# Three plain and accumulating loads per seven-product block move to GpSimd's queue

## The chip, the core and the metric

The kernel runs on one core of a Trainium2 chip. The time is the device time of one execution in microseconds, as a median of several runs. The core has engines that run side by side: TensorE (PE) multiplies matrices, VectorE (DVE) and ScalarE (ACT) work element by element, GpSimd (POOL) and SyncE (SP) here do little but issue DMA transfers. Transfers that SP issues go through the DMA queue q1 (hardware_dynamic in the profile), those that POOL issues through q0 (software_dynamic). Both queues use the same 16 DMA engines.

## The reference

One layer of a hybrid decoder in float32, with 256 tokens of width 2048: a gated feed-forward network (FFN1) at half weight, a token mixer, a second feed-forward network (FFN2), and a last normalisation.

```python
def swiglu_ffn(x, w_gate, w_up, w_down):
    return (jax.nn.silu(x @ w_gate) * (x @ w_up)) @ w_down
...
    x = x + FFN_RESIDUAL_SCALE * swiglu_ffn(rms_norm(x, ffn1_norm[l]),
                                            ffn1_w_gate[l], ffn1_w_up[l], ffn1_w_down[l])
    z = rms_norm(x, mix_norm[l]) @ w_in[l]
...
    x = x + y @ w_out[l]
    x = x + FFN_RESIDUAL_SCALE * swiglu_ffn(rms_norm(x, ffn2_norm[l]),
                                            ffn2_w_gate[l], ffn2_w_up[l], ffn2_w_down[l])
return rms_norm(x, final_norm)
```

The feed-forward width is 5632, so each of the six large matrices holds 46 MB. Left out above is what turns z into y: a gated linear recurrence (RG-LRU) and a short convolution.

## The kernel before

**Numbers.** Each float32 factor is split in two parts, hi and lo, and a product is hi·hi + lo·hi + hi·lo. For a weight block of 1 MB (128 partitions x 4 x 512 numbers), `load` (lines 159 to 168) has SP fetch it into a buffer called raw; `parts_of` (lines 180 to 190) then has ACT cast it to hi in two pieces and DVE compute lo = raw − hi; PE multiplies. A raw buffer is free for the next load when DVE is through with lo. The streamed blocks share three such buffers.

**Stages.** Each feed-forward network has five steps s = 0 to 4, each with a gate block (names g1_s or g2_s, the first number is that of the network) and an up block (u1_s, u2_s); after s = 0, 2 and 4 a down product follows (d1_1, d1_5, d1_9, and d2_... alike). Between the networks the mixer runs, which the change does not touch.

**Seven products.** `seven` (line 396) computes a product of 2 x 2 blocks of weights with seven instead of eight block products. For that it needs sums of weight blocks: w12 + w11, then + w22, then − w11, then + w21. Two more buffers, tagged "kept", hold what lives through the block: `run` is the running sum, `w11` the first block. The start of `run` is made by the DMA itself: SP loads w12 (line 412, through `get`), and then POOL issues an accumulating load (line 413) that adds w11 to what stands in the buffer. Then SP loads w11 again by itself into the other kept buffer (line 414). The remaining blocks (`b2`, `w22`, `b3`, `a2`, `w21`, `a3`) are streamed by SP through the three raw buffers. In the names of buffers 01 is w12 and `run`, 00 is w11, 11 is w22, 10 is w21, and 21, 31, 20, 30 are b2, b3, a2, a3. Down blocks have other first digits (raw_d2_1_11 is the running sum of d2_1, raw_d2_1_10 its w11).

The products go in the order: `run` (p4), w11 (p0), b2, `run` + w22 (p5), b3, run − w11 (p6), w22 (p2), a2, run + w21 (p3), a3, w21 (p1). PE takes 12 or 24 matmuls for each.

**Order and waits.** The scheduler of the framework sets the order of instructions on each engine from the program's order and the dependencies; each engine and each issuing queue works strictly in its order. `run` takes the kept buffer that is free after p6 of the previous block, w11 the one free after its p3. The accumulate waits until the plain load of `run` has landed. The first gate block of FFN1 has its inputs in place already (`ready`); the other 25 calls of `seven` take the path that the change touches: 9 gate, 10 up and 6 down blocks.

After each gate and up block, the result is transposed by DMA: `part` (line 203) has SP issue a transposing transfer from the buffer `pair`, so these stand in SP's queue among the loads.

Of the kernel before, what the change touches and what calls it, by code (L numbers as in the profile page):

```python
# [10 lines left out]
F32 = mybir.dt.float32  # L11
# [3 lines left out]
ALU = mybir.AluOpType  # L15
AX = mybir.AxisListType

P = 128
# [6 lines left out]
CW = 512  # L25
NC_D = D // CW
UK = 4
# [22 lines left out]
def hybrid_block(ctx: ExitStack, tc: tile.TileContext, a: dict, out: bass.AP):  # L50
    nc = tc.nc
# [31 lines left out]
    def bank(name):  # L83
        return psum.tile([P, 512], F32, tag="ps", name=name)

    def f32(ap):
        return ap.bitcast(F32)
# [68 lines left out]
    extra = []  # L156
    turn_of = {"split": 0}

    def load(src, name, pieces=((0, UK),), loaded=None, kept=False):
        if kept:  # L160
            raw = extra[1].tile([P, UK, CW], F32, tag="kept", name=f"raw_{name}", bufs=2)
        else:
            raw = raws.tile([P, UK, CW], F32, tag="raw", name=f"raw_{name}")
        for i, e in pieces:
            nc.sync.dma_start(raw[:, i:e, :], src[i * P : e * P].rearrange("(j p) c -> p j c", p=P))
            if loaded:
                loaded(i)
        return raw

    def splits_of(name):  # L170
        pool, bufs = splits, 2
        if extra:
            turn_of["split"] += 1
            if turn_of["split"] % 3 == 0:
                pool, bufs = extra[0], 1
        hi = pool.tile([P, UK, CW], F32R, tag="hi", name=f"hi_{name}", bufs=bufs)
        lo = pool.tile([P, UK, CW], F32R, tag="lo", name=f"lo_{name}", bufs=bufs)
        return hi, lo, [(hi[:, j, :], lo[:, j, :]) for j in range(UK)]

    def parts_of(raw, name, pieces=((0, 2), (2, UK)), split=None):  # L180
        hi, lo, blk = splits_of(name)
        for i, e in pieces:
            if split:
                split(i)
            act.copy(hi[:, i:e, :], raw[:, i:e, :])
            if split:
                dve.tensor_tensor(lo[:, i:e, :], raw[:, i:e, :], f32(hi[:, i:e, :]), op=ALU.subtract)
        if not split:
            dve.tensor_tensor(lo, raw, f32(hi), op=ALU.subtract)
        return blk  # L190
# [4 lines left out]
    def stationary(tile, t):  # L195

        return [(tile[:, j, t * P : (t + 1) * P], tile[:, j, S + t * P : S + (t + 1) * P]) for j in range(UK)]
# [33 lines left out]
    def multiply(targets, blk, apart=False, middle=None):  # L231


        more = dict(skip_group_check=True) if apart else {}
        for ps, st, begin, _ in targets:
            for j in range(UK):
                pe.matmul(ps, st[j][0], blk[j][0], start=begin and j == 0, stop=False, **more)
                pe.matmul(ps, st[j][1], blk[j][0], start=False, stop=False, **more)
        if middle:
            middle()  # L240
        for ps, st, _, end in targets:
            for j in range(UK):
                pe.matmul(ps, st[j][0], blk[j][1], start=False, stop=end and j == UK - 1, **more)
        if len(targets) == NT:
            onward()
# [150 lines left out]
    def seven(w, rows, cols, sf, xs, name, keep, done, between=None, ready=None, whole=True, seeded=True):  # L396


        a, c, e, d = (bank(f"ps_{name}_{n}") for n in "aced")

        def of(u, n):
            return w[u * UK * P : (u + 1) * UK * P, cols[n] : cols[n] + CW]

        def get(u, n, kept=False):
            return load(of(u, n), f"{name}_{u}{n}", kept=kept)

        (r0, r1), two = rows, len(xs) > 1
        if ready:
            w11, first = ready
            run = get(r0, 1, True)  # L410
        else:
            run, first = get(r0, 1, True), None
            nc.gpsimd.dma_start(run, of(r0, 0).rearrange("(j p) c -> p j c", p=P), accum_op=ALU.add)
            w11 = get(r0, 0, True)
        b2, w22 = get(xs[0][0], 1), get(r1, 1)
        b3 = get(xs[1][0], 1) if two else None
        a2, w21 = get(xs[0][0], 0), get(r1, 0)
        a3 = get(xs[1][0], 0) if two else None

        def snap(ps, n, sign=1.0):  # L420
            s = keep(f"{n}_{name}")
            act.activation(s, ps, AF.Copy, scale=sign)
            return s

        def product_of(i, raw, ps, begin=False, end=True, blk=None):
            multiply([(ps, sf[i], begin, end)], blk or parts_of(raw, f"{name}_p{i}"), True)

        def usual(i, raw, n, *targets):

            blk = parts_of(raw, f"{name}_x{i}{n}")  # L430
            multiply([(ps, stationary(xs[i][1], t), b, z) for ps, t, b, z in targets], blk, True)

        def corner():
            product_of(0, w11, a, True, blk=first)
            if whole:
                act.copy(d, a)
                return []
            return [snap(a, "s1")]

        if ready:  # L440
            s1 = corner()
            hi, lo, blk = splits_of(f"{name}_p4")
            for i in (0, 2):
                o = slice(i, i + 2)
                dve.tensor_tensor(run[:, o], run[:, o], w11[:, o], op=ALU.add)
                act.copy(hi[:, o], run[:, o])
            for i in (0, 2):
                o = slice(i, i + 2)
                dve.tensor_tensor(lo[:, o], run[:, o], f32(hi[:, o]), op=ALU.subtract)
            product_of(4, run, c, True, blk=blk)  # L450
            s5 = [snap(c, "s5")]
        else:
            product_of(4, run, c, True)
            if seeded:
                act.copy(e, c)
            s5 = [] if seeded else [snap(c, "s5")]
            s1 = corner()
        if between:
            between(0)
        usual(0, b2, 1, (e, 1, not seeded, not two), (c, 0, False, False))  # L460
        if between:
            between(1)
        dve.tensor_tensor(run, run, w22, op=ALU.add)
        product_of(5, run, a)
        u2 = snap(a, "u2", -1.0)
        if between:
            between(2)
        if two:
            usual(1, b3, 1, (e, 1, False, True), (c, 0, False, False))
        dve.tensor_tensor(w11, run, w11, op=ALU.subtract)  # L470
        product_of(6, w11, a)
        u3 = snap(a, "u3", -1.0)
        done(1, 1, e, [u3] + s5)
        product_of(2, w22, c)
        done(0, 1, c, [u2])
        usual(0, a2, 0, (d, 0, not whole, False), (a, 1, False, False))
        dve.tensor_tensor(run, run, w21, op=ALU.add)
        product_of(3, run, a, end=not two)
        if two:
            usual(1, a3, 0, (a, 1, False, True), (d, 0, False, False))  # L480
        done(1, 0, a, [])
        product_of(1, w21, d)
        done(0, 0, d, s1)

    def ffn(tag, norm, after, opening=False):
        with (
# [252 lines left out]
            def down(last):  # L739
# [64 lines left out]
                if tag == 1 and m == 5:  # L804
                    prepare()
                seven(
                    wd, (m, n), (2 * CW, CW), sh, [(u, hidden[u]) for u in others], f"d{tag}_{m}", keep, add,
                    within,
# [419 lines left out]
```

## Time and profile before

| | |
|---|---|
| time, median of 3 runs | 1800.07 us (1798.57 to 1800.27) |
| the profiled execution's own time | 1805.48 us |
| its span, first to last instruction | 1803.7 us |
| mean granted TensorE clock | 0.984 |
| PE busy | 1725.1 us (96%) |
| DVE, ACT, POOL busy | 1380.5, 1204.4, 38.8 us |
| loads from SP | 261 of the feed-forward weights, 1 MB each, median 6.1 to 7.0 us from issue to landing |
| accumulating loads from POOL | 25, 1 MB each, median 11.6 to 12.9 us |

How to read the rows. A group of instructions has its line, engine and operation, then what it writes and reads, and how often it occurs. In a timeline a row begins with the start and the length in microseconds and ends, in brackets, with the idle time ahead of it and what ended this. In a list of waits the numbers are the total, the count, and the longest. "DMA to landing" is the time from the issue of a transfer to its end, smallest, median and largest. PEclk is the granted clock, where 1 is full speed. Nearly all rows name line 43, that of a helper that records every operation, so the names of the buffers tell the places.

### The profile page before, as it was taken

To read this page: it belongs to the slowest core of one execution; us is meant where nothing else is said; L and a number is where in the kernel's file an instruction comes from. 1 tells how busy PE (TensorE), PEld (TensorE's weight loads), DVE (VectorE), ACT (ScalarE), POOL (GpSimd) and SP (SyncE) were. 2 spreads that over 40 slices of the span, in tenths; PEclk is the share of its full clock that TensorE was granted. 3 is DMA by queue.
4 is the path that set the end of the run, shared out by engine and by line. 5 is a ranking of instruction groups with operands and counts; after the bars stand their busy time and mean duration, and the time that the engine had idled before them with its cause. 6 is when DMAs were issued, how large, how long until landed. Compare 5 with 4: busy or idle time off the path is not lost.

```text
span 1803.7 us, 19492 instructions
## 1 busy us (share of the span) xinstructions
PE 1725.1 (96%) x7471; PEld 1405.2 (78%) x7471; DVE 1380.5 (77%) x1118; ACT 1204.4 (67%) x1501; POOL 38.8 (2%) x45
## 2 busy tenths in 40 slices
PE   8999998999998989999999999899999999999998
PEld 6887787878876777888888887677778778878786
DVE  8977877768767758768696669769868687778686
ACT  7857566665556657877777776666657574667574
POOL 1000000000000000000000000000000000000000
PEclk9999999999999999999999999999999999999999
DMA  8776677795667684775666695696768668677863
GB/s 305 203 224 203 210 243 201 246 252 164 224 210 200 216 234 159 230 244 187 209 199 210 197 293 164 198 257 184 255 194 247 201 203 257 210 221 222 234 209 117
DMA packets 267373, 389.32 MB, mean 216 GB/s; under 512 B 86292, under 2 KB 88720, under 8 KB 267152
## 3 DMA queue, kind: packets, MB, share of 16 engines
q1 hardware_dynamic: 253616, 360.75, 62.1%
q0 software_dynamic: 13520, 26.29, 8.4%
q8 instruction: 58, 0.95, 0.2%
q10 hardware_dynamic: 144, 1.05, 0.1%
q14 instruction: 35, 0.29, 0.0%
HBM read 366.03 MB, written 2.10 MB: 204 GB/s over the span
## 4 chain that ended last, share of the span: by engine, by line
PE 64%; DMA 15%; DVE 9%; ACT 6%; issue 5%; SPq 0%; DVEq 0%; ACTq 0%
PE ps_in L43 11%; PE ps_d L43 10%; PE ps_g_a L43 6%; DMA raw_u<-in_ffn_w_up_dram 5%; PE ps_g_c L43 5%; PE ps_u_c L43 4%; DMA raw_g<-in_ffn_w_gate_dram 4%; DMA u_g<-pair 4%; PE ps_o L43 4%; PE ps_d_a L43 3%; PE ps_g_e L43 3%; PE ps_g_d L43 3%; PE ps_u_e L43 3%; PE ps_u_a L43 3%; PE ps_d_c L43 3%
## 5 line engine op out<-in xcount | busy, mean ns | idle before, releaser
L43 ACT CAST hi_u_p<-raw_u 128x1024 fp32r<-128x1024 f32 x140 | 143.8, 1044 | 92.6 <-DMA raw_u<-in_ffn_w_up_dram 36.5
L43 DVE TENSOR_TENSOR lo_u_p<-raw_u,hi_u_p 128x2048 fp32r<-128x2048 f32 x70 | 160.0, 2286 | 34.3 <-ACT hi_u_p L43 33.6
L43 ACT CAST hi_g_p<-raw_g 128x1024 fp32r<-128x1024 f32 x136 | 137.4, 1045 | 55.9 <-PE ps_g_a L43 16.4
L43 PE MATMUL ps_d<-hi_d,h 128*128 128x512 f32 x704 | 172.0, 397 | 1.9 <-ACT hi_d L43 1.9
L43 DVE TENSOR_TENSOR lo_g_p<-raw_g,hi_g_p 128x2048 fp32r<-128x2048 f32 (+1 forms) x69 | 155.1, 2254 | 17.6 <-ACT hi_g_p L43 17.2
L43 PEld LDWEIGHTS ps_d<-hi_d,h 128*128 128x128 f32 x704 | 135.6, 193 | 31.7 <-ACT hi_d L43 2.8
L43 PE MATMUL ps_in<-hi_in,xT_nm 128*128 128x512 f32 x640 | 152.3, 390 | 0.1
L43 ACT CAST hi_u_x<-raw_u 128x1024 fp32r<-128x1024 f32 x80 | 82.2, 1046 | 88.2 <-DMA raw_u<-in_ffn_w_up_dram 60.3
L43 PEld LDWEIGHTS ps_in<-hi_in,xT_nm 128*128 128x128 f32 x640 | 119.4, 188 | 25.1 <-ACT hi_in L43 0.6
L43 DVE TENSOR_TENSOR lo_u_x<-raw_u,hi_u_x 128x2048 fp32r<-128x2048 f32 x40 | 91.4, 2286 | 46.4 <-ACT hi_u_x L43 46.4
L43 DVE TENSOR_TENSOR lo_in<-raw_in,hi_in 128x2048 fp32r<-128x2048 f32 x40 | 91.2, 2286 | 43.0 <-ACT hi_in L43 42.6
L43 ACT CAST hi_g_x<-raw_g 128x1024 fp32r<-128x1024 f32 x80 | 80.6, 1044 | 49.3 <-PE ps_g_c L43 17.8
L43 DVE TENSOR_TENSOR lo_d<-raw_d,hi_d 128x2048 fp32r<-128x2048 f32 x44 | 100.5, 2287 | 16.4 <-ACT hi_d L43 16.4
L43 DVE TENSOR_TENSOR lo_g_x<-raw_g,hi_g_x 128x2048 fp32r<-128x2048 f32 x40 | 91.3, 2283 | 25.9 <-ACT hi_g_x L43 25.9
L43 ACT CAST hi_d_p<-raw_d 128x1024 fp32r<-128x1024 f32 x84 | 85.2, 1045 | 35.0 <-PE ps_d_a L43 9.7
L43 ACT CAST hi_d<-raw_d 128x1024 fp32r<-128x1024 f32 x88 | 88.6, 1044 | 17.6 <-DMA raw_d<-in_ffn_w_down_dram 9.3
L43 DVE TENSOR_TENSOR raw_u<-raw_u,raw_u 128x2048 f32<-128x2048 f32 x30 | 68.7, 2291 | 40.9 <-DMA raw_u<-in_ffn_w_up_dram 40.6
L43 DVE TENSOR_TENSOR lo_d_p<-raw_d,hi_d_p 128x2048 fp32r<-128x2048 f32 x42 | 95.8, 2285 | 4.9 <-ACT hi_d_p L43 4.8
L43 ACT CAST hi_in<-raw_in 128x1024 fp32r<-128x1024 f32 x80 | 80.8, 1046 | 26.9 <-PE ps_in L43 21.9
L43 PE MATMUL ps_d<-lo_d,h 128*128 128x512 f32 x352 | 87.2, 389 | 0.0
L43 DVE TENSOR_TENSOR h<-pair,h 128x512 fp32r<-128x512 f32 x44 | 30.3, 689 | 71.5 <-ACT h L43 71.3
L43 PE MATMUL ps_in<-lo_in,xT_nm 128*128 128x512 f32 x320 | 79.0, 389 | 0.0
(405 smaller groups left out, 3716.6 us busy)
## 6 DMA issues: line engine op xcount, KB each, us to landing
raw_d<-in_ffn_w_down_dram SPq DMA_DIRECT2D x88, 1024.0 KB, 6.1
raw_u<-in_ffn_w_up_dram SPq DMA_DIRECT2D x87, 1024.0 KB, 7.0
raw_g<-in_ffn_w_gate_dram SPq DMA_DIRECT2D x86, 1024.0 KB, 6.3
raw_in<-in_w_in_dram SPq DMA_DIRECT2D x40, 1024.0 KB, 5.1
raw_o<-in_w_out_dram SPq DMA_DIRECT2D x16, 1024.0 KB, 5.2
raw_u<-in_ffn_w_up_dram POOLq DMA_DIRECT2D x10, 1024.0 KB, 11.6
raw_g<-in_ffn_w_gate_dram POOLq DMA_DIRECT2D x9, 1024.0 KB, 12.9
raw_d<-in_ffn_w_down_dram POOLq DMA_DIRECT2D x6, 1024.0 KB, 12.6
```

The costliest lines, as they stand in the source:

```text
L43: ins = getattr(self.engine, name)(*args, **kwargs)
```

## The change

The three transfers for the kept buffers are issued by POOL, in this order: the plain load of w12 into the running sum, the accumulating load of w11 onto it, the plain load of w11. SP's queue holds all the others. The waits on buffers are the same as before, and so is the arithmetic.

```diff
         else:
-            run, first = get(r0, 1, True), None
-            nc.gpsimd.dma_start(run, of(r0, 0).rearrange("(j p) c -> p j c", p=P), accum_op=ALU.add)
-            w11 = get(r0, 0, True)
+            run, first = extra[1].tile([P, UK, CW], F32, tag="kept", name=f"raw_{name}_sum", bufs=2), None
+            for n, how in ((1, {}), (0, dict(accum_op=ALU.add))):
+                nc.gpsimd.dma_start(run, of(r0, n).rearrange("(j p) c -> p j c", p=P), **how)
+            w11 = extra[1].tile([P, UK, CW], F32, tag="kept", name=f"raw_{name}_first", bufs=2)
+            nc.gpsimd.dma_start(w11, of(r0, 0).rearrange("(j p) c -> p j c", p=P))
         b2, w22 = get(xs[0][0], 1), get(r1, 1)
```

SP's order where block u1_1 of FFN1 ends and g1_2 begins (u1_1's last loads, 20, 10 and 30, then g1_2's first; L208 is the transposing transfer), before:

```order
L165 DMA raw_u1_1_20_1855<-in_ffn1_w_up_dram 128x4x512
L165 DMA raw_u1_1_10_1857<-in_ffn1_w_up_dram 128x4x512
L165 DMA raw_g1_2_01_2123<-in_ffn1_w_gate_dram 128x4x512
L165 DMA raw_u1_1_30_1859<-in_ffn1_w_up_dram 128x4x512
L165 DMA raw_g1_2_21_2128<-in_ffn1_w_gate_dram 128x4x512
L208 DMA_TRANSPOSE u3_g1_1_1720<-pair_107 128x8x128
L165 DMA raw_g1_2_00_2126<-in_ffn1_w_gate_dram 128x4x512
L165 DMA raw_g1_2_11_2130<-in_ffn1_w_gate_dram 128x4x512
```

and in the changed kernel:

```order
L165 DMA raw_u1_1_20_1855<-in_ffn1_w_up_dram 128x4x512
L165 DMA raw_u1_1_10_1857<-in_ffn1_w_up_dram 128x4x512
L165 DMA raw_u1_1_30_1859<-in_ffn1_w_up_dram 128x4x512
L165 DMA raw_g1_2_21_2128<-in_ffn1_w_gate_dram 128x4x512
L208 DMA_TRANSPOSE u3_g1_1_1720<-pair_107 128x8x128
L165 DMA raw_g1_2_11_2130<-in_ffn1_w_gate_dram 128x4x512
```

The loads of g1_2's running sum (01) and of its w11 (00) are gone from SP's queue; the rest keeps its order.

POOL's order over the same place, with the block before and the one behind, before:

```order
L413 DMA raw_u1_1_01_1844<-in_ffn1_w_up_dram 128x4x512
L413 DMA raw_g1_2_01_2123<-in_ffn1_w_gate_dram 128x4x512
L413 DMA raw_u1_2_01_2410<-in_ffn1_w_up_dram 128x4x512
```

and now (x2 is the plain load with the accumulate behind it):

```order
L414 DMA raw_u1_1_sum_1844<-in_ffn1_w_up_dram 128x4x512 x2
L416 DMA raw_u1_1_first_1847<-in_ffn1_w_up_dram 128x4x512
L414 DMA raw_g1_2_sum_2123<-in_ffn1_w_gate_dram 128x4x512 x2
L416 DMA raw_g1_2_first_2126<-in_ffn1_w_gate_dram 128x4x512
L414 DMA raw_u1_2_sum_2410<-in_ffn1_w_up_dram 128x4x512 x2
L416 DMA raw_u1_2_first_2413<-in_ffn1_w_up_dram 128x4x512
```

POOL had one transfer per block and now has three; w11's load stands behind the accumulate.

SP's order behind block u2_0, where the down product of FFN2 begins (d2_1_0_2 and d2_1_3_0 are single blocks of it), before:

```order
L165 DMA raw_d2_1_0_0_8457<-in_ffn2_w_down_dram 128x4x512
L208 DMA_TRANSPOSE u3_g2_0_8050<-pair_107 128x8x128
L165 DMA raw_d2_1_10_8650<-in_ffn2_w_down_dram 128x4x512
L165 DMA raw_d2_1_0_2_8494<-in_ffn2_w_down_dram 128x4x512
L208 DMA_TRANSPOSE u2_g2_0_7989<-pair_107 128x8x128
L165 DMA raw_d2_1_3_0_8532<-in_ffn2_w_down_dram 128x4x512
```

and now:

```order
L165 DMA raw_d2_1_0_0_8457<-in_ffn2_w_down_dram 128x4x512
L208 DMA_TRANSPOSE u3_g2_0_8050<-pair_107 128x8x128
L208 DMA_TRANSPOSE u2_g2_0_7989<-pair_107 128x8x128
L165 DMA raw_d2_1_0_2_8494<-in_ffn2_w_down_dram 128x4x512
L165 DMA raw_d2_1_3_0_8532<-in_ffn2_w_down_dram 128x4x512
```

Here the second transpose moves ahead of a load as well, and w11 of d2_1 (raw_d2_1_10) no longer stands in front of it. PE's order is the same in both kernels.

## The prediction

> **What bounds the kernel now.** I read the engines' busy time first, then the chain of waits, then what TensorE waited for.
>
> ```profile
> span 1803.7 us, 19492 instructions
> PE 1725.1 (96%) x7471; PEld 1405.2 (78%) x7471; DVE 1380.5 (77%) x1118; ACT 1204.4 (67%) x1501; POOL 38.8 (2%) x45
> ...
> PE 64%; DMA 15%; DVE 9%; ACT 6%; issue 5%; SPq 0%; DVEq 0%; ACTq 0%
> ...
> PE ps_u_a L43 <- ACT hi_u_x L43: 11.7, 8, 2.8
> ```
>
> TensorE (PE) is the bound: 96% of the span, so at most 78.6 us of idle time can be won, plus what a lowered clock costs. The largest waits name ACT, but ACT itself was waiting. One stall, at 284 us, shows for what:
>
> ```profile
> L165 SPq DMA_DIRECT2D raw_u<-in_ffn_w_up_dram x1: 367/367/367, 274.8 to 274.8; - x1
>   ACT hi_u_x L43: 10.6, 1
> DMA to landing us min/median/max: 10.8/10.8/10.8
> ...
> 273.77 1.28 POOL L413 DMA_DIRECT2D raw_g<-in_ffn_w_gate_dram  x1 [38.52 <-DMA raw_g<-in_ffn_w_gate_dram]
> ...
> 286.83 1.20 PE L43 MATMUL ps_u_a<-hi_u_x,x 128*128 128x512 f32 x4 [2.45 <-ACT hi_u_x L43]
> ```
>
> Block u1_1's last streamed load (`a3`, named raw_u1_1_30) is issued by SP at 274.8, 1.0 us behind the accumulating load that POOL issued at 273.77 for the next block. It needs 10.8 us; ACT waits for it, and PE for ACT. Six places have this form, and one table prices them:
>
> ```profile
> 283.00:293.00 10.00, 6.85 (x23) 0.83 0.86 253
> 505.00:512.00 7.00, 5.33 (x22) 1.00 0.82 312
> 603.00:611.00 8.00, 6.99 (x31) 1.00 0.86 299
> 645.00:657.00 12.00, 8.95 (x32) 0.86 0.84 254
> 1343.00:1354.00 11.00, 8.67 (x25) 0.70 0.80 245
> 1431.00:1440.00 9.00, 5.86 (x19) 0.81 0.70 213
> sum 57.00, PE 42.64; mean PE 7.11
> ```
>
> The columns are the stretch, its length, PE's busy time, the granted clock, DMA share and GB/s. PE is idle 57.00 − 42.64 = 14.4 us there, and the clock below 1 costs 10×0.17 + 12×0.14 + 11×0.30 + 9×0.19 = 8.4 us: 22.8 us together.
>
> Why is the load slow? While both transfers run, the engines give the two queues the same number of packets, and the accumulate's packets are the dearer ones:
>
> ```profile
> q0 software_dynamic: 477, 0.95, 64.6%
> q1 hardware_dynamic: 548, 1.10, 40.9%
> ```
>
> (window 277 to 285 us). That is not so when the streamed load is nearer behind the accumulate. Two like places, near the end and in the middle:
>
> ```profile
> L165 SPq DMA_DIRECT2D raw_u<-in_ffn_w_up_dram x1: 367/367/367, 1685.4 to 1685.4; - x1
> DMA to landing us min/median/max: 6.0/6.0/6.0
> ...
> 1684.96 1.29 POOL L413 DMA_DIRECT2D raw_d<-in_ffn_w_down_dram  x1 [38.82 <-DMA raw_d<-in_ffn_w_down_dram]
> ...
> L165 SPq DMA_DIRECT2D raw_u<-in_ffn_w_up_dram x1: 367/367/367, 1333.6 to 1333.6; - x1
> DMA to landing us min/median/max: 11.4/11.4/11.4
> ...
> 1332.51 1.30 POOL L413 DMA_DIRECT2D raw_g<-in_ffn_w_gate_dram  x1 [39.34 <-DMA raw_g<-in_ffn_w_gate_dram]
> ```
>
> 0.4 us behind the accumulate the load lands after 6.0 us; 1.1 us behind it, after 11.4. The load that comes early enough goes first and the accumulate waits. Between 0.4 and 1.0 us lies a point of decision, and the change moves the accumulate by about that much.
>
> **The change, part by part.** 25 blocks are touched (10 up, 9 gate, 6 down); 50 plain loads leave SP for POOL.
>
> *1. The running sum's plain load starts later.* POOL starts later behind what it waits for than SP does. The plain load of g1_2 shows by how much:
>
> ```profile
> L165 SPq DMA_DIRECT2D raw_g<-in_ffn_w_gate_dram x1: 368/368/368, 267.1 to 267.1; - x1
> DMA to landing us min/median/max: 6.0/6.0/6.0
> ```
>
> It lands at 273.1 and POOL's instruction begins at 273.77: 0.65 us. The plain load inherits this, and so does the accumulate behind it. Where does it show?
>
> ```profile
> L413 POOL DMA_DIRECT2D raw_u<-in_ffn_w_up_dram x10: 1292/1293/1372, 79.8 to 1644.8; - x10
>   ACT hi_u_p L43: 32.1, 7
> DMA to landing us min/median/max: 10.3/11.6/13.8
> ...
>   ACT hi_g_p L43: 10.8, 2
> ...
> 335.35 2.00 ACT L43 CAST hi_u_p<-raw_u 128x1024 fp32r<-128x1024 f32 x2 [4.79 <-DMA raw_u<-in_ffn_w_up_dram]
> ...
> 340.48 0.84 PE L43 MATMUL ps_u_c<-hi_u_p,xs 128*128 128x512 f32 x3
> ...
> 1153.91 2.94 ACT L43 CAST hi_u_p<-raw_u 128x1024 fp32r<-128x1024 f32 x3 [7.66 <-DMA raw_u<-in_ffn_w_up_dram]
> ...
> 1155.01 2.14 PE L43 MATMUL ps_u_c<-hi_u_p,xs 128*128 128x512 f32 x8 [0.79 <-ACT hi_u_p L43]
> ```
>
> ACT waited for the accumulate in 7 + 2 = 9 of the 25 blocks; in the other 16 it landed early. In most of the nine PE still has work in front: at 335.35 ACT begins the cast, and PE reaches the product at 340.48 without a wait, a cover of some 3 us after the two casts of 2.00. At 1155.01 there is none, and 0.65 us comes straight through: **+0.7**. Without the covers it would be 9 × 0.65 = +5.9; with cover everywhere 0.
>
> *2. The streamed load gets in front.* The accumulate starts at least 0.65 us later, and the streamed load keeps its time, since it waits for its own buffer. The distances 1.0 and 1.1 become 0.35 and 0.45, below or at the 0.4 that gave 6.0 us. Landing about 4 us earlier ends all six waits. Not all of 22.8 us need come back: behind the load stand two casts and the next block's transfers, now delayed. I take 70%: **−16** (0 to −22.8).
>
> *3. The accumulate then lands later.* It moves from the lower to the upper end of its 10.3 to 13.8 us, some 2 us, plus the 0.65. The 16 loose blocks cover it, the tight ones mostly do with their 3 us: **+1** (0 to 5 × 2.65 = +13).
>
> *4. The first block's weights (w11) stand behind the accumulate* in POOL's queue, where SP used to send them in parallel. At g2_1:
>
> ```profile
> L165 SPq DMA_DIRECT2D raw_g<-in_ffn_w_gate_dram x3: 367/368/368, 1252.4 to 1258.0; - x3
> DMA to landing us min/median/max: 11.1/11.2/11.3
> ...
> 1266.44 2.00 ACT L43 CAST hi_g_p<-raw_g 128x1024 fp32r<-128x1024 f32 x2 [1.49 <-DMA raw_g<-in_ffn_w_gate_dram]
> ...
> 1274.66 2.89 PE L43 MATMUL ps_g_e<-hi_g_x,x 128*128 128x512 f32 x8 [2.12 <-ACT ps_g_e L43]
> ```
>
> Three streamed loads, w11 the second of them, are issued 2.8 us apart and land as far apart. Behind the accumulate, w11 changes places with the third: about 2.5 us later. ACT stands still for w11 at 1266.44, behind it queue the casts and the copy that PE awaits at 1274.66, so 2 of the 2.5 come through here and at g1_1, which has the same pattern after its down product: **+4**. If no tight block covered it: 9 × 2.5 = +22; if DVE's wait for the third load, now earlier, is the last, 0.
>
> *5. The clock.* A wait that has been 2.12 us grows past the 2.45 of 286.83, behind which the clock was 0.83 over 10 us: 1.7 us each, at two places: **+3.4** (0 to 9 × 1.7 = +15). The Trainium skill's "TensorE: Matmul & The Clock Gate", section "Why this matters for your kernels", asks for an idle gap above about 3 us before the clock drops; by that this term would be 0. The row at 286.83 disagrees.
>
> *6. SP's queue is relieved* of a quarter-hundred plain loads between streamed loads and transposes. In the stretch that follows u1_4:
>
> ```profile
> 668.80 3.01 PE L43 MATMUL ps_d<-hi_d,h 128*128 128x512 f32 x12 [1.38 <-ACT hi_d L43]
> DMA to landing us min/median/max: 7.9/7.9/7.9
> ```
>
> The transpose issued at 655.5 took 7.9 us behind a w11, and 1.38 us of PE's time followed; similar at one or two more: **−2** (0 to −4).
>
> Sum: 0.7 − 16 + 1 + 4 + 3.4 − 2 = −8.9. The profiled execution took 1805.48 us, so 1796.6 for its like; the runs' median of 1800.07 stands 5.4 lower, so **1791**. All good ends give −26.8, all bad ones +56, which cannot all hold together.
>
> **The rivals.**
>
> *A, the order does not matter (17%).* The two queues share packet by packet from wherever they are, so the streamed load still takes 11 us. For it speak the equal counts 477 and 548; against it, the 6.0 us at 1685.4. Terms 1, 3, 4, 5, 6 remain: +7.1, so 1807. The Trainium skill's "DMA: Bandwidth & Descriptors", section "Queues, rings and completion order", states this rule: each DMA engine goes round-robin between queues at packet granularity. By it the load at 1685.4 should have taken about as long as that at 1333.6, and it did not.
>
> *B, POOL's one queue makes tight blocks late (13%).* Plain data then accumulate then w11 in a row, and none of the nine blocks hides w11: term 4 is +22 from the point at which w11 lands more than the 3 us of cover late, and term 5 follows with some +9. With the gain of term 2 kept: 0.7 − 16 + 1 + 22 + 9 − 2 = +14.7, so 1815. For it: ACT already waits in all nine. Against: w22's earlier arrival covers a part.
>
> *C, nothing to be told from no change (17%).* The six stalls shrink by a third to a half (−9), because the next transfers become late, and terms 1 and 3 to 6 give +7: 1798. Below 0.2%, 3.6 us, this kernel's measurement cannot tell a change.
>
> *D, more (8%).* Term 2 whole, terms 3 to 5 hidden: 0.7 − 22.8 − 2 = −24, so 1776.
>
> That the queue stays as it was is excluded: the instructions stand on POOL in the changed program.
>
> **How the numbers follow.** The forecast with its own range 1780 to 1796 has 45%. Faster is forecast plus D, 53%; same is C, 17%; slower is A and B, 30%. The range for 8 in 10 runs from D to B, 1776 to 1816; outside it are the further ends of D and B.
>
> **What would show it.** Term 2: raw_u1_1_30 lands within 8 us, and the waits of PE at 284, 646, 1344 and 1432 are gone; if its time stays near 11, rival A holds. Term 1: POOL's plain loads land in 5 to 7.5 us; if they take the 10.3 to 13.8 of the accumulates, every term on POOL grows and the forecast falls. Term 3: accumulates at 12.5 to 14 in nearly all blocks. Term 4: ACT's second wait in g1_1 and g2_1 near 4 us, not 1.49. Term 5: the count of stretches with a low clock, four in the table above, falls; if it rises, B.

## The result and the profile after

The changed kernel takes 1816.28 us (median of 4 runs, 1815.99 to 1819.34) where the kernel before takes 1799.32 us (1796.24 to 1800.27): a ratio of 1.0101, 95% interval 1.0084 to 1.0119. It is 17 us slower, where 9 us less were forecast, and 0.28 us above the upper end, 1816 us, of the range for 8 in 10. One run of e11 below, of 2123.78 us at a granted clock of 0.752 where its three others show 0.991 to 0.998, counts in its median and not in its ratio.

The page of the changed kernel, the lines that answer to those shown of before:

```profile
span 1814.6 us, 19482 instructions
...
PE 1728.3 (95%) x7471; PEld 1407.8 (78%) x7471; DVE 1382.4 (76%) x1118; ACT 1204.2 (66%) x1501; POOL 77.5 (4%) x95
...
q1 hardware_dynamic: 227216, 308.32, 53.4%
q0 software_dynamic: 27120, 78.72, 16.1%
```

The row of q0 before, for comparison:

```profile
q0 software_dynamic: 13520, 26.29, 8.4%
```

The move itself is there: q0 carries 78.7 MB in place of 26.3. That is two more loads of 1 MB in each of the 25 blocks; the accumulate was on POOL's queue already. The profiled execution of the kernel before was itself one of its longer ones, so the spans differ by 10.9 us only, the medians by 17. Of the 10.9, PE's busy time has 3.2 (1725.1 to 1728.3, at a mean granted clock of 0.982 after 0.984), its idle time the other 7.7. What PE waited for, in the changed kernel:

```profile
PE ps_u_d L43 <- ACT hi_u_p L43: 18.8, 10, 6.0
PE ps_u_a L43 <- ACT hi_u_x L43: 15.4, 13, 3.3
PE ps_g_a L43 <- DVE lo_g_p L43: 8.9, 7, 1.8
```

The first of these rows before:

```profile
PE ps_u_d L43 <- ACT hi_u_p L43: 12.7, 8, 3.0
```

The second row is the wait that term 2 wanted to end: 15.4 us where it was 11.7. The first was 12.7 and its longest piece 3.0; now they are 18.8 and 6.0. It belongs to the last product (p1) of an up block.

**One such place,** with the longest wait of the row. The end of u1_2, ahead of the down product d1_5. In the kernel before, the timelines of SP, ACT and PE:

```profile
366.62 0.37 SPq L165 DMA_DIRECT2D raw_d<-in_ffn_w_down_dram  x1
372.16 2.06 SPq L208 DMA_TRANSPOSE u_g<-pair  x1
374.27 1.54 SPq L165 DMA_DIRECT2D raw_d<-in_ffn_w_down_dram  x2
...
379.21 2.26 ACT L43 COPY pair<-u_g 128x1024 uint16<-128x1024 uint16 x2 [5.18 <-DMA u_g<-pair]
...
383.50 1.19 PE L43 MATMUL ps_u_d<-hi_u_p,x 128*128 128x512 f32 x4 [2.98 <-ACT hi_u_p L43]
```

and in the changed kernel, those of POOL, SP, ACT and PE:

```profile
366.61 1.32 POOL L414 DMA_DIRECT2D raw_d_sum<-in_ffn_w_down_dram  x1 [6.28 <-DMA raw_d_sum<-in_ffn_w_down_dram]
373.15 0.77 POOL L416 DMA_DIRECT2D raw_d_first<-in_ffn_w_down_dram  x1 [5.22 <-DVE lo_u_p L43]
...
374.92 3.66 SPq L208 DMA_TRANSPOSE u_g<-pair  x1
...
384.62 2.23 ACT L43 COPY pair<-u_g 128x1024 uint16<-128x1024 uint16 x2 [7.83 <-DMA u_g<-pair]
...
388.89 2.07 PE L43 MATMUL ps_u_d<-hi_u_p,x 128*128 128x512 f32 x4 [5.97 <-ACT hi_u_p L43]
```

ACT works in its order: a copy that waits for a transposing transfer, and behind it the second half of the cast for p1. PE waits for that cast, 2.98 us before and 5.97 us after. The transposing transfer lands 7.0 us after its issue before and 9.6 us after; e14 below, which moves w11 alone, has 9.4 at this place. Before, SP issued d1_5's w11 as one of the two loads at 374.27, behind the transposing transfer in the same queue. After, POOL issues it at 373.15, ahead of the transposing transfer, in the other queue and right behind the accumulate. (All of PE's work is some 2.4 us later here than before.) The stretch from 376 to 384 us shows what the DMA engines then did, before:

```profile
q1 hardware_dynamic: 2440, 2.76, 103.7%
q0 software_dynamic: 45, 0.06, 4.1%
```

and after:

```profile
q0 software_dynamic: 488, 1.46, 60.9%
q1 hardware_dynamic: 1455, 1.05, 48.8%
```

The engines that finished a streamed load and a transpose almost alone now give more than half of their time to POOL's queue. Some of this is the end of the accumulate, which lands at 380.0 us here and at 377.3 before. In the four microseconds behind its landing nearly all of POOL's traffic is w11. Before (377.6 to 381.6) POOL's queue has no packet there, and after (380 to 384) it has this:

```profile
q1 hardware_dynamic: 1185, 0.49, 57.6%
q0 software_dynamic: 218, 0.83, 53.2%
```

The down product's w11 is first read by ACT at 418.54 us, some 34 us behind that stretch.

### The profile page after: what moved, and what is told of

Its sections match the earlier page's. It is cut to its first block, busy times and chain, and to the rows that moved or that the text cites. A ratio compares the mean times of both kernels' runs of the same rounds, so it can differ in the third digit from the quotient of the medians.

```text
span 1814.6 us, 19482 instructions
## 1 busy us (share of the span) xinstructions
PE 1728.3 (95%) x7471; PEld 1407.8 (78%) x7471; DVE 1382.4 (76%) x1118; ACT 1204.2 (66%) x1501; POOL 77.5 (4%) x95
## 5 line engine op out<-in xcount | busy, mean ns | idle before, releaser
L43 ACT CAST hi_u_p<-raw_u_sum 128x1024 fp32r<-128x1024 f32 x60 | 61.7, 1045 | 53.2 <-DMA raw_u_sum<-in_ffn_w_up_dram 34.2
L43 DVE TENSOR_TENSOR lo_u_p<-raw_u_sum,hi_u_p 128x2048 fp32r<-128x2048 f32 x30 | 68.6, 2286 | 32.9 <-ACT hi_u_p L43 32.9
L43 DVE TENSOR_TENSOR raw_u_sum<-raw_u_sum,raw_u 128x2048 f32<-128x2048 f32 x20 | 45.8, 2292 | 44.6 <-DMA raw_u<-in_ffn_w_up_dram 44.6
L43 ACT COPY pair<-u_g 128x1024 uint16<-128x1024 uint16 x40 | 46.7, 1192 | 47.0 <-DMA u_g<-pair 44.3
L43 PEld LDWEIGHTS ps_d<-lo_d,h 128*128 128x128 f32 x352 | 66.1, 188 | 13.7
L43 ACT CAST hi_g_p<-raw_g_sum 128x1024 fp32r<-128x1024 f32 x54 | 55.2, 1044 | 28.4 <-DVE raw_g_sum L43 8.3
L43 PEld LDWEIGHTS ps_in<-lo_in,xT_nm 128*128 128x128 f32 x320 | 60.1, 188 | 12.4
```

The lines of the kernel that those rows point to most:

```text
L43: ins = getattr(self.engine, name)(*args, **kwargs)
```

## The experiments

Theory S says: w11 now starts long before it is needed, and takes DMA time from the streamed loads and transposes that are needed at once. Theory T names the place where S becomes time: the transposes and ACT behind them. Rival L: the sum's plain load makes all behind it late. Rival N: the nine tight blocks, whose products wait for their own transfers, are late. Ratios below are to the kernel before, run on the same chip.

### Each half alone

```diff
 # e1: run's plain load on POOL, w11 = get(r0, 0, True) stays
+            run = extra[1].tile([P, UK, CW], F32, tag="kept", name=f"raw_{name}_01", bufs=2)
+            nc.gpsimd.dma_start(run, of(r0, 1).rearrange("(j p) c -> p j c", p=P))
 # e2: run = get(r0, 1, True) stays, w11's plain load on POOL behind the accumulate
+            w11 = extra[1].tile([P, UK, CW], F32, tag="kept", name=f"raw_{name}_00", bufs=2)
+            nc.gpsimd.dma_start(w11, of(r0, 0).rearrange("(j p) c -> p j c", p=P))
```

> Half of the change alone: the running sum's plain load goes to POOL, the accumulate stays there, w11 stays with SP. Theory S (w11's early transfer on POOL's queue takes half of the DMA engines from the streamed loads, and causes the loss): close to before, 1796 to 1802 us. Theory L (the running sum's plain load on POOL makes everything behind it late): most of the loss is here, 1808 to 1816 us.

> The other half alone: only w11's plain load goes to POOL, behind the accumulate; the running sum's plain load stays with SP. Theory S: nearly the whole loss, 1810 to 1818 us, and the streamed load behind the accumulate (21 of the next block) lands after 13 to 14 us instead of 11 to 12. Theory L: 1798 to 1803 us.

Measured: e1 1805.79 us, 1.0028 (1.0008 to 1.0048). e2 1821.31 us, 1.0106 (1.0066 to 1.0146). So w11's move carries the loss, some 3 us above S's range; the sum's plain load adds little, though 4 us more than S allowed. The two add up to more than the whole change. PE's waits in the two:

```profile
PE ps_u_a L43 <- ACT hi_u_x L43: 17.2, 14, 2.2
PE ps_g_a L43 <- DVE lo_g_p L43: 10.2, 7, 2.2
```

are the largest of e1, and of e2 this one:

```profile
PE ps_u_d L43 <- ACT hi_u_p L43: 44.4, 10, 6.6
```

### The accumulate started later

This tests term 2 by itself: the accumulate behind the streamed load, nothing else moved.

```diff
             run, first = get(r0, 1, True), None
+            nc.gpsimd.tensor_copy(run[:, 0, :256], run[:, 0, :256])
             nc.gpsimd.dma_start(run, of(r0, 0).rearrange("(j p) c -> p j c", p=P), accum_op=ALU.add)
```

> The kernel before, with a small POOL copy (128x256 of the running sum onto itself) between the running sum's plain load and the accumulate, so that the accumulate starts later by that copy. If the point of decision between 0.4 and 1.0 us is real, the block's last streamed load (30) lands in 6 to 8 us in nearly all blocks and the time falls to 1784 to 1794 us. If the order does not matter, 1800 to 1806 us and the load still takes 10 to 12 us.

Measured: 1802.58 us, 1.001 (0.9988 to 1.0031). Neither expectation holds whole: the load lands early, as the first had it, and the time stays where the second put it. The profile says why. The place at 284 us again, in e3: POOL's timeline, the streamed load 30 of u1_1, then ACT and PE.

```profile
277.17 1.28 POOL L414 DMA_DIRECT2D raw_g<-in_ffn_w_gate_dram  x1 [0.42 <-POOL raw_g L413]
...
L165 SPq DMA_DIRECT2D raw_u<-in_ffn_w_up_dram x1: 368/368/368, 276.5 to 276.5; - x1
...
DMA to landing us min/median/max: 5.5/5.5/5.5
...
291.59 2.26 ACT L43 COPY pair<-u_g 128x1024 uint16<-128x1024 uint16 x2 [5.55 <-DMA u_g<-pair]
...
295.37 1.20 PE L43 MATMUL ps_u_d<-hi_u_p,x 128*128 128x512 f32 x4 [2.71 <-ACT hi_u_p L43]
```

The same copy of ACT before:

```profile
290.56 2.24 ACT L43 COPY pair<-u_g 128x1024 uint16<-128x1024 uint16 x2 [0.94 <-DMA u_g<-pair]
```

The streamed load, now ahead of the accumulate, lands after 5.5 us instead of 10.8, and PE's wait of 2.45 for it is gone. So the order decides, as the prediction said. But the accumulate's own time on the engines remains. ACT comes to its copy early and waits 5.55 us for the transposing transfer there, where it waited 0.94 us before; PE then waits 2.71 us for p1's cast. The gain is given back one product later.

### The transposes on another queue

```diff
-        held["turn"] = nc.sync.dma_start(turned.rearrange("p (r c) -> p r c", c=P), two, transpose=True)
+        held["turn"] = nc.scalar.dma_start(turned.rearrange("p (r c) -> p r c", c=P), two, transpose=True)
```

in the kernel before (t1), in the changed kernel (t2), and in e3 (t3).

> The kernel before, but all transposing transfers are issued by ACT instead of SP, so that none stands behind a streamed load in SP's queue. Theory T (the loss comes through the transposes: they stand behind a streamed load that shares the engines with POOL's queue, and ACT, held by their result, makes PE wait): 1785 to 1797 us, since the kernel before has these waits too, only shorter. Rival B (streamed loads are late everywhere): 1796 to 1804 us.

> The changed kernel, with the transposing transfers on ACT's queue as in the run beside it. Theory T: within 6 us of that run, where the same change costs 17 us with transposes on SP. Rival B: 12 to 20 us above it.

> The kernel before with the small POOL copy that starts the accumulate later, and the transposing transfers on ACT's queue. If the streamed load's gain was given back at the transposes only, this is below both of its parts: 1775 to 1788 us. If it was given back elsewhere too, as the run with the transposes moved alone, within 4 us.

Measured: t1 1863.08 us, 1.0348 (1.0307 to 1.0388); t2 1867.29 us, 1.0373 (1.0309 to 1.0436); t3 1879.02 us, 1.0429 (1.0402 to 1.0457). All three are some 60 to 80 us slower, and t1 is outside both of its ranges. t3 is too: it stands 16 us above t1, neither below its parts nor within 4 us of t1. Two lines of t1 where the first up block ends:

```profile
126.03 2.04 ACTq L208 DMA_TRANSPOSE u_g<-pair  x1
...
140.00 2.23 ACT L43 COPY pair<-u_g 128x1024 uint16<-128x1024 uint16 x2 [9.84 <-DMA u_g<-pair]
```

So a transposing transfer can be late, here by 13.9 us, with no load ahead of it in its queue, and shared DMA engines fit what is seen. Over the 20 transfers u_g the median fell all the same, from 6.9 us before to 5.5 in t1, so these runs do not rule out that the place in SP's queue has a part. T's forecast for t1 falls. t2 stands 4 us above t1, as T expected, but with intervals of 0.4 and 0.6% and a base 63 us slower this decides nothing.

### w11 held back on POOL

In the changed kernel, POOL issues w11 only behind a one-column copy of the block's first streamed load (b2); the issue itself is not new, it moves down.

```diff
+        b2 = get(xs[0][0], 1)
+        if not ready:
+            nc.gpsimd.tensor_copy(w11[:, 0, :1], b2[:, 0, :1])
+            nc.gpsimd.dma_start(w11, of(r0, 0).rearrange("(j p) c -> p j c", p=P))
```

> The changed kernel, but POOL issues w11 only when the block's first streamed load (b2) has landed: a one-column copy of b2 into w11's buffer, which the transfer then overwrites, stands before it. Theory S (w11's early start takes bandwidth from what is needed sooner): 1800 to 1808 us, with streamed loads behind the accumulate back at 11 to 12 us. If the software queue itself is the cost: 1812 to 1820 us.

Measured: 1865.57 us, 1.0346 (1.0316 to 1.0376). Outside both expectations. What ACT waited for:

```profile
ACT hi_g_p L43 <- DMA raw_g_first<-in_ffn_w_gate_dram: 49.3, 6, 15.2
ACT hi_u_p L43 <- DMA raw_u_first<-in_ffn_w_up_dram: 47.1, 9, 8.0
```

96 us of waits for w11 itself: held until b2 has landed, it is too late for its own product. The run says nothing on S. It does show that w11 cannot simply be moved back everywhere.

### The change by kinds of blocks

```diff
-        else:
+        elif name[0] == "d":    # e5; e6 has name[0] != "d"
+            run, first = extra[1].tile([P, UK, CW], F32, tag="kept", name=f"raw_{name}_sum", bufs=2), None
...
+        else:
             run, first = get(r0, 1, True), None
...
```

> The change in the six down blocks alone; gate and up blocks as before. Theory T (the loss is at the ends of up blocks, where a following block's transfers on POOL's queue delay the streamed load and the transposes behind it): four up blocks before a down product lost 1.4 to 5.4 us each in the profile of the changed kernel, so +6 to +12 us, 1806 to 1812. Rival N (the loss is in the nine tight gate and up blocks, whose own sums and w11 come late): within 3 us of before.

> The change in the 19 gate and up blocks alone; down blocks as before. Theory T: the rest of the 17 us, +5 to +10 us, 1805 to 1810. Rival N: nearly all of it, +14 to +18 us.

Measured: e5 1806.37 us, 1.0043 (1.0026 to 1.0060); e6 1808.44 us, 1.0053 (1.0031 to 1.0075). The six down blocks, none of them tight, carry 0.43 of some 0.96%, as T expected, and N did not. The 19 others still mix tight and loose blocks.

### w11 alone, in the tight and in the loose blocks

This separates S from N: the kernel before, with only w11's plain load on POOL, in the nine tight blocks (e13) or in the other 16 (e14).

```diff
+            if name in ("u1_0", "g1_1", "u1_1", "u1_2", "u2_0", "g2_1", "u2_1", "u2_2", "u2_4"):   # e14: not in
+                w11 = extra[1].tile([P, UK, CW], F32, tag="kept", name=f"raw_{name}_00", bufs=2)
+                nc.gpsimd.dma_start(w11, of(r0, 0).rearrange("(j p) c -> p j c", p=P))
+            else:
+                w11 = get(r0, 0, True)
```

> Only w11's plain load on POOL, and only in the nine tight blocks, whose products wait for the accumulate; the sum's plain load and all other w11 loads stay with SP. Theory S (in loose blocks w11 starts long before it is needed, and takes bandwidth from streamed loads and transposes that are needed at once): 1798 to 1803 us. Rival N (w11 behind the accumulate is late for its own product in the tight blocks): 1810 to 1818 us.

> Only w11's plain load on POOL, and only in the other 16 blocks. Theory S: 1808 to 1820 us, with the first streamed load of a down product (d_0) after 12 to 14 us instead of 11, and PE's wait for the last product's cast (ps_u_d for hi_u_p) above 25 us in all. Rival N: 1797 to 1802 us.

Measured: e13 1800.84 us, 1.0004 (0.9987 to 1.0021); e14 1816.66 us, 1.0092 (1.0067 to 1.0118). So w11's move costs nothing that can be told from zero in the tight blocks, and in the loose ones, whose products do not wait for it, about as much as the whole change: for w11 N falls, and what S says of the place of the loss holds.

The landing times show it across the kernel. In the loose blocks, SP's loads issued 2 to 4 us behind an accumulate landed after 10.6 to 12.8 us before (15 loads) and 10.6 to 12.4 in e13 (12 loads). With w11 on POOL's queue it is 12.8 to 15.3 in e14 and 12.8 to 14.6 in the changed kernel (14 loads each). In e14 the first streamed load of d1_5, which took 11.4 us before, takes this, and PE's wait behind it in all:

```profile
DMA to landing us min/median/max: 13.1/13.1/13.1
...
PE ps_u_d L43 <- ACT hi_u_p L43: 32.1, 12, 6.4
```

### No accumulating load at all

If the accumulate's time on the DMA engines stands behind the stalls, a kernel without it should win. w11 is loaded plainly anyway, so an engine can add it; the product with w11 (p0) goes first, to give the add time.

```diff
             run, first = get(r0, 1, True), None
-            nc.gpsimd.dma_start(run, of(r0, 0).rearrange("(j p) c -> p j c", p=P), accum_op=ALU.add)
             w11 = get(r0, 0, True)
+            nc.gpsimd.tensor_tensor(run, run, w11, op=ALU.add)      # e7, e9; in e10: dve.tensor_tensor
...
+            s1 = corner()            # e7, e10; e9 keeps it behind product_of(4, ...)
             product_of(4, run, c, True)
             if seeded:
                 act.copy(e, c)
             s5 = [] if seeded else [snap(c, "s5")]
-            s1 = corner()
```

> No accumulating load at all: SP loads w12 and w11 plainly, POOL adds w11 to the running sum with an elementwise instruction, and the product with w11 goes before that with the sum. If the accumulate's cost on the DMA engines is what makes the streamed loads and transposes late, 1770 to 1790 us. If POOL's add takes longer than the 8 to 12 us that the accumulate takes, or disturbs DVE, 1800 to 1830 us.

> No accumulating load, POOL adds, but the product with the sum (p4) stays ahead of the product with w11 (p0), as in the kernel before. If the gain of 38 us is the accumulate's absence alone, 1758 to 1766 us; if the new order of these two products carries part of it, 1770 to 1790 us.

> No accumulating load, DVE adds w11 to the sum instead of POOL, p0 ahead of p4. 25 adds of 2.29 us are 57 us more on DVE; POOL's adds made DVE's own 1118 instructions 85 us longer. If what matters is DVE's total, 1752 to 1762 us; if DVE's place in line matters (the add stands among the instructions that PE waits for), 1765 to 1785 us.

> The same kernel as the run with DVE's add, on the same chip as the run beside it, so that the two can be set against each other: 1733 to 1739 us.

Measured: e7 1760.87 us, 0.9782 (0.9755 to 0.9808). e9 1785.2 us, 0.9921 (0.9891 to 0.9951). e10 1735.86 us, 0.9641 (0.9604 to 0.9679), and again 1735.22 us, 0.964 (0.9619 to 0.966). All beat the kernel before, e10 by 62 us. e7 and e10 are faster than either of their expectations, e9 lies in its second. The new order of the two products carries a good part in e7 (0.978 against 0.992 without it), and in the new order DVE is the better place for the add. No run has the new order with the accumulate kept, so how much of e10's gain belongs to the accumulate alone stays open; e9, in the old order and with POOL's add, has 0.8%. e10's page, and its largest wait of PE:

```profile
span 1735.0 us, 19443 instructions
...
PE 1696.9 (98%) x7471; PEld 1391.6 (80%) x7471; DVE 1435.4 (83%) x1143; ACT 1207.0 (70%) x1501; POOL 6.3 (0%) x20
...
PE ps_g_a L43 <- ACT hi_g_p L43: 6.6, 6, 1.8
```

The waits that led the list before (12.7 us of ps_u_d for hi_u_p, 11.7 of ps_u_a for hi_u_x) are no longer among the largest. PE's idle time is 38.1 us in place of 78.6, and its busy time is 28 us shorter with the same 7471 matmuls, at a mean granted clock of 0.999 in place of 0.984.

### The plain loads on POOL, with no accumulate in the kernel

```diff
-            run, first = get(r0, 1, True), None
-            w11 = get(r0, 0, True)
+            run, first = extra[1].tile([P, UK, CW], F32, tag="kept", name=f"raw_{name}_sum", bufs=2), None
+            nc.gpsimd.dma_start(run, of(r0, 1).rearrange("(j p) c -> p j c", p=P))
+            w11 = extra[1].tile([P, UK, CW], F32, tag="kept", name=f"raw_{name}_first", bufs=2)
+            nc.gpsimd.dma_start(w11, of(r0, 0).rearrange("(j p) c -> p j c", p=P))
```

in e7 (that is e8) and in e10 (e11).

> No accumulating load, POOL adds as in the run that had 1761 us, and the two plain loads (w12 and w11) on POOL's queue as in the change. Theory S (POOL's queue costs because an accumulate and w11 run one behind the other on it, against the streamed loads): with no accumulate there the same move costs little, 1757 to 1768 us. If the software queue itself is what costs, the 17 us come back: 1774 to 1784 us.

> As the run with DVE's add (1736 us, no accumulate, both loads on SP), but the two plain loads on POOL's queue, where nothing else of POOL's work stands between them. Theory S (it takes an accumulate on that queue): 1733 to 1742 us. If the queue itself costs, as the run with POOL's add and POOL's loads hints (12 us): 1745 to 1755 us.

Measured: e8 1773.24 us, 0.985 (0.9818 to 0.9883), against 0.9782 with the loads on SP. e11 1763.63 us, 0.9795 (0.9767 to 0.9823), against 0.964 for its partner on the same chip. e8 lies between its two ranges, e11 above both of its own. The form of S put on record here, that the loss takes an accumulate on POOL's queue, falls. Without the accumulate, w11 is on the path of every block, since the add waits for both loads. So what the pair adds is that moving these two loads to POOL's queue costs 0.7% (e8) and 1.5% (e11) in kernels where products wait for them at once. Whether it is the shared engines again or POOL's queue itself was not separated, and no run moves w11 to a second queue other than POOL's.

## Why the prediction was wrong

*Term 2, the streamed load in front (−16): this step failed, twice.* First, the accumulate does not start later against the streamed load in five of the six places. The same place in the changed kernel, POOL's timeline and the load 30 of u1_1:

```profile
268.52 0.75 POOL L414 DMA_DIRECT2D raw_g_sum<-in_ffn_w_gate_dram  x1 [27.72 <-DVE lo_u_p L43]
275.04 1.34 POOL L414 DMA_DIRECT2D raw_g_sum<-in_ffn_w_gate_dram  x1 [5.76 <-DMA raw_g_sum<-in_ffn_w_gate_dram]
...
L165 SPq DMA_DIRECT2D raw_u<-in_ffn_w_up_dram x1: 367/367/367, 276.6 to 276.6; - x1
...
DMA to landing us min/median/max: 10.1/10.1/10.1
```

The load stands 1.6 us behind the accumulate, not 0.35 as predicted and not even the 1.0 of before. The plain load was issued at 268.52 and landed 6.1 us later, at 274.6, and POOL began the accumulate 0.4 us after that, where the prediction carried over the 0.65 us seen before. In 22 of the 25 blocks this lag was 0.29 to 0.42 us. Against PE, the accumulate even began earlier: 4.0 us ahead of the product at 279.01, where before it was 2.3 us ahead of the same product at 276.06. The distance was taken as "before plus the lag", though both ends of it move. The point of decision itself is real: before, SP's loads issued 0.02 to 0.74 us behind an accumulate land after 5.7 to 8.3 us (6 loads), those 0.93 to 1.46 us behind it after 10.3 to 11.6 (14 loads). In the other places of the six the distance is 1.22 to 1.41 us and the load takes 9.9 to 11.8, except one (603 us before), where it is 0.47 and 6.2. Of the four waits of PE that were to go, two shrank, to 0.54 and 0.90 us (at 288 and 653), and two remain, with 3.30 and 2.71 (at 1355 and 1446). Second, where the order was really turned (e3), the load landed after 5.5 us as promised, and still nothing was won, since the next thing that ACT needs, the transposed block, comes through the same engines. The prediction named what stands behind the load, two casts and the next block's transfers, and took 30% off; it should have asked at what time the next wait ends. That time had hardly moved: ACT's copy began at 290.56 in the kernel before, after a wait of 0.94 us, and at 291.59 in e3, where PE stood 1.9 us later.

*Term 6, SP relieved (−2): wrong sign, and the main loss.* It counted what leaves SP's queue and not where it goes. The bytes of w11 stay on the same 16 engines; in SP's queue they came behind what was needed sooner, in POOL's they come beside it. This is the loss in the main: e14, with w11 alone in the loose blocks, has +0.92%, some 16.5 us (12 to 21), where the whole change has 17. The prediction's own row held the key, the equal packet counts of the two queues, and it was used for the accumulate only.

*Term 4, w11 late in the tight blocks (+4), and rival B.* e13 measures it: 1.0004, nothing outside its interval of −0.13 to +0.21%. In the changed kernel ACT's waits for w11 in g1_1 and g2_1 are 2.5 and 2.1 us, not near 4. The price of B, 1815 us, agrees with the result to a microsecond by luck. Its mechanism is wrong for w11, whose move costs nothing measurable in the tight blocks; what the sum's loads add there is at most e1's part.

*Term 3, the accumulate lands later (+1).* It does not: the 25 accumulates land after 10.0 to 15.1 us (median 11.9), before after 10.3 to 15.0 (median 12.1).

*Term 1, the sum's plain load (+0.7).* With the accumulate behind it, e1 measures +0.28%, 1.4 to 8.6 us; the size was too small. Where these microseconds stand is open: PE's waits in e1 show more for hi_u_x and for lo_g_p, less for hi_u_p, and their sum does not settle it.

*Term 5, the clock (+3.4).* PE's busy time with the same matmuls is 3.2 us longer in the profiled execution. About the size, by luck in part. Of the two places named, g1_1 did get a lowered clock (0.91 from 205 to 224 us, before 1.00), and g2_1 lost the one it had (1.00 from 1280 to 1295, before 0.89 from 1270 to 1285).

*Rival A* (the order does not matter) falls with e3: 5.5 us against 10.8 for the same load. In the changed kernel the load stayed near 11 us, as A said, but since the order was not turned. In e3, POOL's queue moved 3 packets and SP's 509 from the accumulate's issue at 277.17 to 281 us, and 267 against 209 from 282 to 286. So the near-even sharing weighed beside A describes, for these transfers, only the stretch in which both are under way.

## What to carry to other kernels

Moving a transfer to another queue does not take it off the DMA engines: it takes it out of its place in line. Ask of each moved transfer when it is needed, and what needed sooner stood ahead of it in the old queue. When a stall is to be ended, look for the time at which the next wait ends, before booking the gain. And an accumulating load of 1 MB, which lands only after 10 to 15 us here, may be dearer than an add of 2.29 us on an engine with 23% of its time free: e10 has both this and a new order of products, and gains 3.6%.

## What had not been expected

POOL's elementwise add slows DVE. The same 70 instructions of DVE, first in the kernel before, then in e7, and one group of POOL's adds in e7:

```profile
L43 DVE TENSOR_TENSOR lo_u_p<-raw_u,hi_u_p 128x2048 fp32r<-128x2048 f32 x70 | 160.0, 2286 | 34.3 <-ACT hi_u_p L43 33.6
...
L43 DVE TENSOR_TENSOR lo_u_p<-raw_u,hi_u_p 128x2048 fp32r<-128x2048 f32 x70 | 225.6, 3223 | 46.1 <-ACT hi_u_p L43 46.1
...
L414 POOL TENSOR_TENSOR raw_u<-raw_u,raw_u 128x2048 f32<-128x2048 f32 x10 | 54.9, 5485 | 489.6 <-DMA raw_u<-in_ffn_w_up_dram 489.6
```

Of DVE's instructions over 2 us, the 45 that overlap an add of POOL take 4.35 us on average in e7, the others 2.48. DVE's busy time grew from 1380.5 to 1465.8 us with the same 1118 instructions: 85 us, more than doing the 25 adds on DVE itself, for which e10 then showed 55 us (1435.4). And the small copy of 128x256 numbers that POOL made in e3 took 1.95 us:

```profile
274.80 1.95 POOL L413 COPY raw_g<-raw_g 128x256 f32<-128x256 f32 x1 [37.51 <-DMA raw_g<-in_ffn_w_gate_dram]
```

That the transposing transfers, with nothing but a change of the issuing queue from SP to ACT, would cost 63 us was not expected either; the runs do not say how much of it comes from ACT's time for issuing and how much from the transfers' own.
